# Turning the memory queries with VectorE blocks and an exchange, and issuing two exchanges from GpSimd in four parts

## The chip, the cores and the metric

The kernel runs on one core of a Trainium2 chip. The core's engines run side by side, each through its own list of instructions in order, and wait for one another by semaphores: TensorE (PE; matrix products and its own kind of transpose), VectorE (DVE), ScalarE (ACT), GpSimd (POOL) and SyncE (SP). SyncE and GpSimd issue the DMA transfers of this kernel, each into a queue of its own, and 16 DMA engines carry out both. The metric is the time of one execution on the device in microseconds; lower is better.

## The reference

Two layers of a bidirectional encoder over 512 positions of width 2048. Each layer norms its input, makes one wide input projection, cuts that into the inputs of three parallel groups of heads and a gate, and projects the gated result back:

```python
for l in range(DEPTH):
    h = rmsnorm(x, pre_norm_g[l])
    z = h @ w_in[l]
    q_lat, kv_lat, k_pe, gb, gc, xin, q_mem, gate = split_cols(z)
    ...
    a_out = mla_attention(q, k, v)
    c_out = short_gated_conv(gb, gc, xin, conv_w[l])
    mem_n = rmsnorm(mem, mem_norm_g[l])
    m_out = memory_attention(q_mem.reshape(b, s, MEM_HEADS, MEM_HEAD_DIM), mem_n, w_mk[l], w_mv[l])
    y = jnp.concatenate([a_out, c_out, m_out], axis=-1) * jax.nn.silu(gate)
    o = y @ w_o[l]
    x = x + rmsnorm(o, post_norm_g[l])
```

`memory_attention` takes the queries `q_mem` (512 positions, 4 heads of 128) to 256 memory tokens: scores, softmax, and the weighted sum of the values. `short_gated_conv` is `gb * conv3(gc * xin)`, a convolution of width 3 over positions. All of it is float32.

## The kernel before

**Products.** A float32 matrix is split into a high part and a rest (`wh` and `wl` for weights, lines 189 and 190), and each product is done as three matmuls: high by high, high by rest, rest by high (lines 272 to 274 of `mm3`). TensorE takes the positions in four tiles of 128.

**Input projection.** For each layer it is done in five groups of columns, 0 to 4, each by a scheme with seven products of half-size blocks in place of eight (P1 to P7, called passes). A group needs sums and differences of weight blocks: some are formed on VectorE (line 178), others by loads that add to what lies in the buffer already. The groups that matter here:

- group 2 makes the gate `gm` and the memory queries `qm` (512 columns each);
- group 3, tile `lat`, makes the latents of the multi-head attention, 2 x 416 columns, in 28 steps of one weight tile each (about 281 to 345 us in layer 0 and 1007 to 1071 us in layer 1); VectorE also works out the tables of the rotary positions beside it in layer 0 (`tables`, `tables_wide`, `tables_turned`; lines 327 to 357);
- group 4 makes the gates `ga` (2 x 512 columns; 345 to 432 us and 1071 to 1158 us); beside its later steps the latents are normed and turned.

**Order.** `Program` holds a list of steps: a step names its weight units and a function. `put` adds the steps of passes, `add` a function without weights, and `weave(steps, extra, every, n)` puts n of the extra steps behind every so many steps. In `run` (lines 124 ff.) the loads of weight units run ahead of the step by a fixed number of units: a plain load goes out on SyncE's queue, an accumulating one (`more`, line 146 on GpSimd) goes to GpSimd's, behind the step that has used the buffer's first contents. There are 8 raw buffers `wr`, and 3 each of `wh` and `wl`; a cast waits until one of the three is free, that is until TensorE is through with it. Work on VectorE may be placed by the scheduler a little away from where the program has it; that is seen in the rows below.

**Blocks and exchanges.** Tiles in `BLOCKS` hold a row of positions by channels laid out so that VectorE can turn 32x32 blocks in place (`blocks_turned`, line 935: STREAM_TRANSPOSE). What then is still missing of a whole transpose is a swap of blocks among the four quarters of the partitions; `exchange` (lines 937 to 943) does it with 16 DMAs of 32x4x128 elements, 64 KB each, from the source tile to a slab. `gate_rows` does so for the gates and `conv_rows` for the result of the convolution, `cy`, into a slab `y`. In all of them SyncE issues the DMAs. The convolution ends on VectorE in line 987 (`cy` times `gb`), and its exchange comes into the program behind the third step of group 3.

**Memory queries.** `qm` isn't among the blocks. `qm_turn` (lines 998 to 1006) turns it by TensorE: for each of the four heads four transposes into a PSUM bank (`turn4`, line 917, tile `tps`), from which ScalarE takes the scaled high part `QmH` (line 1004) and VectorE the rest `QmL` (line 1005). The four turns, and seven turns of latents, are woven into group 4, two behind each second step from its seventeenth on.

Of the kernel before, what the change touches and what calls it, by code (L numbers as in the profile page):

```python
# [5 lines left out]
F32 = mybir.dt.float32  # L6
# [52 lines left out]
PI_DOWN = 3.1415925  # L59

RAW, PIECES, SLABS = 8, 4, 19
BLOCKS = "gc", "gb", "gm", "ga0", "ga1"


class Unit:
# [162 lines left out]
def encoder(tc, x, xt, mem, memt, positions, columns, conv_w, w_in, q_norm_g, w_uq, w_qr, kv_norm_g, w_ukv,  # L228
# [32 lines left out]
    def slab(name, dt=F32):  # L261
        return slabs.tile([P, D], dt, tag="slab", name=nm(name))
# [657 lines left out]
    def y_slab(k):  # L920
        if k not in G["ys"]:
            G["ys"][k] = slab("y").rearrange("p (j c) -> p j c", j=4)
        return G["ys"][k]

    def of_tiles(a):

        return a.rearrange("q (t p j) -> q t p j", t=NT, j=32)

    def in_tiles(a):

        return a.rearrange("q (p t j) -> q t p j", t=NT, j=32)
# [2 lines left out]

        nc.vector.transpose(v, v)

    def exchange(dst, src):


        for p in range(4):  # L940
            for b in range(4):
                a = src[32 * p:32 * p + 32].rearrange("i t (c b) j -> i c b (t j)", b=4)[:, :, b]
                nc.sync.dma_start(dst[32 * b:32 * b + 32, :, P * p:P * p + P], a)  # L943

    def gate_rows(k, name, C):
        def f():
# [45 lines left out]
        turns = [turn(n, t) for n in ("gc", "gb") for t in range(NT)]  # L992
        return [[(f, []) for f in fs] for fs in (turns[:4] + [edges] + turns[4:], [part(c) for c in range(8)], [ends])]

    def conv_rows(C):
        return lambda: exchange(y_slab(2), C["cy"])

    def qm_turn(j, C):
        def f():
            if j == 0:  # L1000
                G["Qm"] = tuple(slab(n, F32R).rearrange("p (i c) -> p i c", i=4) for n in ("QmH", "QmL"))
            ps = turn4(lambda t: C["qm"][:, t], j)
            hi, lo = G["Qm"][0][:, j, :], G["Qm"][1][:, j, :]
            nc.scalar.activation(hi, ps, AF.Copy, scale=SC_MEM)
            nc.vector.scalar_tensor_tensor(lo, ps, SC_MEM, hi.bitcast(F32), op0=ALU.mult, op1=ALU.subtract)
        return f

    def normalise(views, n, gain, by=None):
# [177 lines left out]
    def head_iters(j, rope, src, keys, whole=False):  # L1186
# [50 lines left out]
        def av(b):  # L1237
            def g():
                if b == 0 or whole:
                    st["o"] = bank("o")  # L1240
                VH, VL = src()[1]
                o = st["o"] if whole else st["o"][:, b * 256:(b + 1) * 256]
                PT = st.pop("PT" if whole else ("PT", b))
                for k in range(kts):
                    mm3(o, (VH(k), VL(k)), (PT[0][:, k], PT[1][:, k]), k == 0, k == kts - 1)
                if b == 1:
                    y = G["ys"][j // 4][:, j % 4, :]
                    nc.vector.tensor_tensor(in_tiles(y), of_tiles(st["o"]), in_tiles(y), op=ALU.mult)
            return g
        return [((score(t), [], 0.4), trans(t), av(t // 2) if t == 3 or t == 1 and not whole else None, 4 if whole and kts > 2 else 5)  # L1250
                for t in range(NT)]
# [250 lines left out]
    for l in range(depth):  # L1502
# [111 lines left out]
        put(gs[2][1], weave(gs[2][2], turns, 1), weave(gs[2][3] + gs[2][4], parts, 1))  # L1614
        add(owns[3])
        put(gs[3][0][:1], ends, gs[3][0][1:3])
        add(conv_rows(C))
        put(gs[3][0][3:])
        steps = [s for passes in gs[3][1:] for s in passes]
        if l == 0:  # L1620
            add(tables)
            steps[16:16] = [(tables_wide, [])]
            steps[20:20] = [(tables_turned, [])]
        put(steps)
        add(owns[4])
        add(lambda l=l: latents_rows(l))
        g4 = [s for steps in gs[4] for s in steps]
        put(g4[:2])
        add(lambda l=l, C=C: latents_begin(l, C))
        put(g4[2:8])  # L1630
        add(lambda C=C: k_rope(C))
        put(g4[8:13])
        add(gate_rows(3, "gm", C))
        put(g4[13:16])
        lat = [latent_turn(l, "cq", j) for j in range(4)] + [latent_turn(l, "ckv", j) for j in range(2)] + [k_rope_turn]
        more = [(f, []) for f in lat + [qm_turn(j, C) for j in range(4)]]
        put(weave(g4[16:], more, 2, 2)[:-2])
        add(mem_fetch)
        add(tables_fetch)
        put(weave(g4[16:], more, 2, 2)[-2:])  # L1640
        G["left"] = Y = Left(False, l + 1 < depth)
        g0, g1, gains, fetch = out_proj(l)

# [81 lines left out]
```

## Time and profile before

| | |
|---|---|
| time, median of 3 runs | 1462.49 us (1461.67 to 1463.37) |
| time of the profiled execution | 1462.12 us |
| its span | 1460.3 us |
| granted TensorE clock | 0.998 |
| GpSimd busy | 271.1 us (19%) |
| q0, the software queue of GpSimd: packets, MB, share of the 16 engines | 56192, 125.39, 42.6% |
| q1, the hardware queue of SyncE: packets, MB, share of the 16 engines | 105184, 170.74, 36.4% |
| y<-cy, 32 pieces of 64 KB in both layers, issue to landing | 4.5 us (median) |
| y<-gm, 32 pieces, issue to landing | 6.6 us (median) |

The profiled execution's time is 1.8 us more than its span. PE is TensorE's matmuls, PEld its weight loads, which lie beside them; a line such as "L190 DVE" is line 190 of the kernel on VectorE. In the rows of a timeline, the bracket at the end tells how long the engine had idled and what ended that. In rows of waits stand the total, the number of waits and the longest, in us. In rows of windows there follow, behind the stretch and its length, the busy time of PE, PEld, DVE, ACT and POOL with counts, the granted clock, the busy share of the DMA engines (1.00 is all 16) and GB/s. "SPq" is time in which SyncE issues DMAs.

### The profile page before, as it was taken

Reading aid. Unit: us, or ns where it says so; the run is one execution under the profiler, and the core shown is the slowest. Engines: PE = TensorE matmul, PEld = TensorE weight load, DVE = VectorE, ACT = ScalarE, POOL = GpSimd, SP = SyncE. Lnnn points to the kernel's source line nnn. Section 1 sums busy time; section 2 is a strip of 40 time slices with the busy share of each in tenths; the row PEclk is TensorE's granted clock in tenths of the full one; section 3 lists DMA queues with packets and bytes.
Section 4 is the critical chain, followed back from the end, with each engine's and each line's share of the span. In section 5 each row is a group of like instructions: output and inputs, shape, how many; then the busy total and the mean of one; then the engine's idle time right before and its main releaser. Section 6 shows DMA issues by size and latency. Waiting matters only on the chain.

```text
span 1460.3 us, 19491 instructions
## 1 busy us (share of the span) xinstructions
PE 1444.3 (99%) x7040; PEld 1231.5 (84%) x7040; DVE 1108.3 (76%) x1529; ACT 870.4 (60%) x1350; POOL 271.1 (19%) x280
## 2 busy tenths in 40 slices
PE   9999999999999999999999999999999999999997
PEld 8888888898888888888898888888988888888886
DVE  5899685977678778868879666759576776788687
ACT  7856344636468688644777434445364686776543
POOL 0032303031301100311210333030313001004111
PEclk9999999999999999999999999999999999999999
DMA  9999969697976382795986999695979664129973
GB/s 368 415 260 220 231 185 206 156 207 215 235 220 181 83 264 87 135 242 148 340 286 224 240 233 227 187 193 157 215 197 239 219 179 114 31 87 159 269 164 130
DMA packets 161472, 297.37 MB, mean 204 GB/s; under 512 B 12288, under 2 KB 51744, under 8 KB 157536
## 3 DMA queue, kind: packets, MB, share of 16 engines
q0 software_dynamic: 56192, 125.39, 42.6%
q1 hardware_dynamic: 105184, 170.74, 36.4%
q8 instruction: 55, 0.90, 0.2%
q14 instruction: 41, 0.34, 0.1%
HBM read 266.05 MB, written 21.63 MB: 197 GB/s over the span
## 4 chain that ended last, share of the span: by engine, by line
PE 89%; DVE 4%; DMA 2%; SPq 2%; issue 1%; ACT 1%; POOL 0%; POOLq 0%; DVEq 0%; ACTq 0%
PE P L273 21%; PE P L274 21%; PE P L272 21%; PE ptp L1233 2%; DVE wl L190 2%; SPq L943 2%; DMA wr<-in_w_in_dram 2%; PE o L273 1%; PE o L272 1%; PE o L274 1%; PE sc L272 1%; PE sc L273 1%; PE sc L274 1%; PE mk L274 1%; PE mk L273 1%
## 5 line engine op out<-in xcount | busy, mean ns | idle before, releaser
L189 ACT CAST wh<-wr 128x1024 fp32r<-128x1024 f32 (+2 forms) x436 | 444.3, 1023 | 438.8 <-PE P L274 311.5
L190 DVE TENSOR_TENSOR wl<-wr,wh 128x1024 fp32r<-128x1024 f32 (+2 forms) x436 | 515.2, 1185 | 240.6 <-ACT wh L189 237.5
L272 PE MATMUL P<-wh,S 128*128 128x512 f32 (+1 forms) x896 | 344.5, 384 | 0.8 <-DVE lat L542 0.4
L273 PE MATMUL P<-wl,S 128*128 128x512 f32 (+1 forms) x896 | 343.6, 384 | 0.6 <-DVE wl L190 0.6
L274 PE MATMUL P<-wh,S 128*128 128x512 f32 (+1 forms) x896 | 343.8, 384 | 0.0
L272 PE MATMUL P<-wh,A 128*128 128x512 f32 (+1 forms) x656 | 252.9, 386 | 2.0 <-ACT wh L189 2.0
L273 PE MATMUL P<-wl,A 128*128 128x512 f32 (+1 forms) x656 | 252.1, 384 | 2.5 <-DVE wl L190 2.5
L274 PE MATMUL P<-wh,A 128*128 128x512 f32 (+1 forms) x656 | 251.8, 384 | 0.0
L146 POOL DMA_DIRECT2D wr<-in_w_in_dram x132 | 158.2, 1198 | 438.8 <-DVE wl L190 258.4
L272 PEld LDWEIGHTS P<-wh,S 128*128 128x128 f32 x896 | 168.2, 188 | 31.5 <-DVE lat L542 0.8
L273 PEld LDWEIGHTS P<-wl,S 128*128 128x128 f32 x896 | 168.2, 188 | 31.0 <-DVE wl L190 0.9
L274 PEld LDWEIGHTS P<-wh,S 128*128 128x128 f32 x896 | 168.2, 188 | 30.0
L273 PEld LDWEIGHTS P<-wl,A 128*128 128x128 f32 x656 | 123.2, 188 | 25.5 <-DVE wl L190 3.7
L272 PEld LDWEIGHTS P<-wh,A 128*128 128x128 f32 x656 | 123.1, 188 | 24.5 <-ACT wh L189 2.7
L274 PEld LDWEIGHTS P<-wh,A 128*128 128x128 f32 x656 | 123.1, 188 | 22.1
L146 POOL DMA_DIRECT2D wr<-in_w_o_dram x40 | 48.3, 1235 | 299.7 <-DVE wl L190 292.8
L1220 ACT ACTIVATE P<-sc,nm 128x512 f32<-128x512 f32 (+1 forms) x96 | 59.9, 624 | 27.7 <-DVE nm L1217 27.4
L1223 ACT ACTIVATE P<-P,rec 128x512 f32<-128x512 f32 (+1 forms) x96 | 62.3, 662 | 7.0 <-DVE rec L1222 7.0
L1217 DVE TENSOR_REDUCE nm<-sc 128x1 f32<-128x512 f32 (+1 forms) x96 | 56.7, 595 | 10.0 <-PE sc L1215 9.0
L178 DVE TENSOR_TENSOR wr<-wr,wr 128x1024 f32<-128x1024 f32 (+1 forms) x36 | 42.3, 1175 | 5.5 <-DMA wr<-in_w_in_dram 5.1
L1233 PE MATMUL ptp<-identr,P 128*128 128x128 f32 x320 | 46.0, 272 | 0.3 <-ACT P L1223 0.3
L1233 PEld LDWEIGHTS ptp<-identr,P 128*128 128x128 f32 x320 | 38.0, 140 | 6.5 <-ACT P L1223 0.7
(323 smaller groups left out, 2081.2 us busy)
## 6 DMA issues: line engine op xcount, KB each, us to landing
wr<-in_w_in_dram SPq DMA_DIRECT2D x128, 512.0 KB, 5.6
wr<-in_w_in_dram POOLq DMA_DIRECT2D x108, 512.0 KB, 7.3
wr<-in_w_o_dram SPq DMA_DIRECT2D x48, 512.0 KB, 6.1
wr<-in_w_o_dram POOLq DMA_DIRECT2D x40, 512.0 KB, 7.2
wr<-in_w_in_dram SPq DMA_DIRECT2D x32, 416.0 KB, 3.8
wr<-in_w_in_dram POOLq DMA_DIRECT2D x24, 416.0 KB, 6.9
wr<-in_w_mk_dram SPq DMA_DIRECT2D x15, 512.0 KB, 8.7
wr<-in_w_mv_dram SPq DMA_DIRECT2D x15, 512.0 KB, 10.1
```

The lines of the kernel that those rows point to most:

```text
L146: engine.dma_start(dst, src, **kw)
L178: nc.vector.tensor_tensor(tiles[a], tiles[a], tiles[b], op=ALU.add)
L189: pin(nc.scalar.copy(hi[:, h], src[:, h]))
L190: pin(nc.vector.tensor_tensor(lo[:, h], src[:, h], hi[:, h].bitcast(F32), op=ALU.subtract))
L272: nc.tensor.matmul(ps, ah, bh, start=first, stop=False, **kw)
L273: nc.tensor.matmul(ps, ah, bl, start=False, stop=False, **kw)
L274: nc.tensor.matmul(ps, al, bh, start=False, stop=last, **kw)
L943: nc.sync.dma_start(dst[32 * b:32 * b + 32, :, P * p:P * p + P], a)
L1217: nc.vector.tensor_reduce(nmax, ps, axis=AX.X, op=ALU.max, negate=True)
L1220: nc.scalar.activation(pt, ps, AF.Exp, bias=nmax, accum_out=tot)
L1223: nc.scalar.activation(pt, pt, AF.Copy, scale=rec)
L1233: nc.tensor.transpose(ps[:, k * P:(k + 1) * P], pt[:, k * P:(k + 1) * P], G["ident"])
```

## The change

Five things are changed in the program of each layer.

1. `qm` joins the blocks. VectorE turns its blocks in place with four transposes of 128x512 (`qm_turn(t, C)`), put at steps 11 to 17 of group 3's later passes, and 16 exchange DMAs bring them into a slab (`qm_rows`), which is also the one that will hold the rest part `QmL`. They are issued by GpSimd in four parts of four, between steps of group 4. Two splits of 1024 columns each (`qm_split`) then take the high and the rest part from that slab in SBUF; the 16 transposes on TensorE and their evictions are gone.
2. The convolution's exchange is issued by GpSimd too, in four parts of four, at the start of group 3.
3. The latent turns and the two splits are woven one behind each step of group 4, and no longer two behind each second one.
4. Two functions of the rotary tables come later among group 3's steps (`tables_wide` from 16 to 22, `tables_turned` from 20 to 26; the six steps put in ahead of them are four block turns and two parts of the exchange, which leaves the two functions within a step of where they were among the weight steps; in VectorE's own order the rope terms of lines 327 to 357 begin two rests `wl` later).
5. The last multiplication of the memory heads by the gate takes `y` as contiguous rows.

```diff
-BLOCKS = "gc", "gb", "gm", "ga0", "ga1"
+BLOCKS = "gc", "gb", "gm", "qm", "ga0", "ga1"
...
-    def exchange(dst, src):
+    def exchange(dst, src, queue=nc.sync, blocks=range(4)):
-        for p in range(4):
+        for p in blocks:
             for b in range(4):
                 a = src[32 * p:32 * p + 32].rearrange("i t (c b) j -> i c b (t j)", b=4)[:, :, b]
-                nc.sync.dma_start(dst[32 * b:32 * b + 32, :, P * p:P * p + P], a)
+                queue.dma_start(dst[32 * b:32 * b + 32, :, P * p:P * p + P], a)
...
-    def conv_rows(C):
-        return lambda: exchange(y_slab(2), C["cy"])
-    def qm_turn(j, C):
+    def conv_rows(p, C):
+        return lambda: exchange(y_slab(2), C["cy"], nc.gpsimd, (p,))
+    def qm_turn(t, C):
+        return lambda: blocks_turned(C["qm"][:, t])
+    def qm_rows(p, C):
         def f():
-            if j == 0:
-                G["Qm"] = tuple(slab(n, F32R).rearrange("p (i c) -> p i c", i=4) for n in ("QmH", "QmL"))
-            ps = turn4(lambda t: C["qm"][:, t], j)
-            hi, lo = G["Qm"][0][:, j, :], G["Qm"][1][:, j, :]
-            nc.scalar.activation(hi, ps, AF.Copy, scale=SC_MEM)
-            nc.vector.scalar_tensor_tensor(lo, ps, SC_MEM, hi.bitcast(F32), op0=ALU.mult, op1=ALU.subtract)
+            if p == 0:
+                C["QmL"] = slab("QmL")
+            exchange(C["QmL"].rearrange("p (i c) -> p i c", i=4), C["qm"], nc.gpsimd, (p,))
+        return f
+    def qm_split(k, C):
+        def f():
+            if k == 0:
+                G["Qm"] = slab("QmH", F32R), C["QmL"]
+            h, (hi, lo) = slice(1024 * k, 1024 * k + 1024), G["Qm"]
+            nc.scalar.activation(hi[:, h], lo[:, h], AF.Copy, scale=SC_MEM)
+            nc.vector.scalar_tensor_tensor(lo[:, h].bitcast(F32R), lo[:, h], SC_MEM, hi[:, h].bitcast(F32),
+                                           op0=ALU.mult, op1=ALU.subtract)
+            if k:
+                G["Qm"] = tuple(a.rearrange("p (i c) -> p i c", i=4) for a in (hi, lo.bitcast(F32R)))
         return f
...
-                    nc.vector.tensor_tensor(in_tiles(y), of_tiles(st["o"]), in_tiles(y), op=ALU.mult)
+                    if rope is None:
+                        nc.vector.tensor_tensor(y, st["o"], y, op=ALU.mult)
+                    else:
+                        nc.vector.tensor_tensor(in_tiles(y), of_tiles(st["o"]), in_tiles(y), op=ALU.mult)
...
-        add(conv_rows(C))
+        add(conv_rows(0, C))
         put(gs[3][0][3:])
+        add(conv_rows(1, C))
         steps = [s for passes in gs[3][1:] for s in passes]
+        for n in (17, 15, 13, 11):
+            steps[n:n] = [(qm_turn((17 - n) // 2, C), [])]
+        steps[2:2] = [(conv_rows(3, C), [])]
+        steps[1:1] = [(conv_rows(2, C), [])]
         if l == 0:
             add(tables)
-            steps[16:16] = [(tables_wide, [])]
-            steps[20:20] = [(tables_turned, [])]
+            steps[22:22] = [(tables_wide, [])]
+            steps[26:26] = [(tables_turned, [])]
...
-        put(g4[2:8])
+        put(g4[2:6])
+        add(qm_rows(0, C))
+        put(g4[6:8])
+        add(qm_rows(1, C))
         add(lambda C=C: k_rope(C))
-        put(g4[8:13])
+        put(g4[8:10])
+        add(qm_rows(2, C))
+        put(g4[10:12])
+        add(qm_rows(3, C))
+        put(g4[12:13])
...
-        more = [(f, []) for f in lat + [qm_turn(j, C) for j in range(4)]]
-        put(weave(g4[16:], more, 2, 2)[:-2])
+        more = [(f, []) for f in lat[:4] + [qm_split(0, C)] + lat[4:6] + [qm_split(1, C)] + lat[6:]]
+        last = weave(g4[16:], more, 1)
+        put(last[:-2])
```

What this moves is seen in the order of the instructions. On SyncE, at the start of group 3 in layer 0 (`wr` are raw weight buffers, loaded 416 columns wide; `y<-cy` is the convolution's exchange), as a piece of the difference:

```order
 L146 DMA wr_2452<-in_w_in_dram 128x2x416
 L146 DMA wr_2470<-in_w_in_dram 128x2x416
-L943 DMA y_2490<-cy_2164 32x4x128 x16
-L146 DMA wr_2507<-in_w_in_dram 128x2x416
-L146 DMA wr_2562<-in_w_in_dram 128x2x416
+L146 DMA wr_2495<-in_w_in_dram 128x2x416
+L146 DMA wr_2558<-in_w_in_dram 128x2x416
```

The weight loads now follow one another; the numbers of the buffers change only in name. On GpSimd at the same place, where the `wr` rows are accumulating loads:

```order
 L146 DMA wr_2041<-in_w_in_dram 128x2x512
 L146 DMA wr_2222<-in_w_in_dram 128x2x416
+L943 DMA y_2490<-cy_2164 32x4x128 x8
 L146 DMA wr_2246<-in_w_in_dram 128x2x416
+L943 DMA y_2490<-cy_2164 32x4x128 x8
 L146 DMA wr_2270<-in_w_in_dram 128x2x416
 L146 DMA wr_2294<-in_w_in_dram 128x2x416
```

The four parts stand as two lots of eight, ahead of the second and of the third accumulating load of group 3. In group 4 of layer 0, still on GpSimd, the queries' exchange stands so in the changed kernel:

```order
L146 DMA wr_2906<-in_w_in_dram 128x2x512
L943 DMA QmL_3208<-qm_1831 32x4x128 x4
L146 DMA wr_2924<-in_w_in_dram 128x2x512
L943 DMA QmL_3208<-qm_1831 32x4x128 x4
L146 DMA wr_2959<-in_w_in_dram 128x2x512
L943 DMA QmL_3208<-qm_1831 32x4x128 x4
L146 DMA wr_2883<-in_w_in_dram 128x2x512
L146 DMA wr_3188<-in_w_in_dram 128x2x512
L943 DMA QmL_3208<-qm_1831 32x4x128 x4
L146 DMA wr_2906<-in_w_in_dram 128x2x512
```

Before, these accumulating loads followed one another without anything between them; now a part of four stands ahead of the third, fourth, fifth and seventh load of the group. On VectorE, where group 3 of layer 0 begins, the rows before were (`wl` are rests of weight tiles, written wl_2429 and so on, which TensorE takes in that order; line 178 sums two raw tiles; line 935 turns blocks):

```order
L190 TENSOR_TENSOR wl_2373<-wr_2222,wh_2372 128x832
L987 TENSOR_TENSOR cy_2164<-cy_2164,gb_867 128x1024
L190 TENSOR_TENSOR wl_2397<-wr_2246,wh_2396 128x832
L178 TENSOR_TENSOR wr_2222<-wr_2222,wr_2322 128x832
L935 STREAM_TRANSPOSE gm_1830<-gm_1830 128x16x32
L178 TENSOR_TENSOR wr_2246<-wr_2246,wr_2370 128x832
L935 STREAM_TRANSPOSE gm_1830<-gm_1830 128x16x32
L190 TENSOR_TENSOR wl_2429<-wr_2270,wh_2428 128x832
L190 TENSOR_TENSOR wl_2455<-wr_2294,wh_2454 128x832
```

and in the changed kernel they are:

```order
L190 TENSOR_TENSOR wl_2373<-wr_2222,wh_2372 128x832
L984 TENSOR_TENSOR cy_2164<-cy_2164,ends_2157 128x16
L935 STREAM_TRANSPOSE qm_1831<-qm_1831 128x16x32
L987 TENSOR_TENSOR cy_2164<-cy_2164,gb_867 128x1024
L190 TENSOR_TENSOR wl_2397<-wr_2246,wh_2396 128x832
L987 TENSOR_TENSOR cy_2164<-cy_2164,gb_867 128x1024
L935 STREAM_TRANSPOSE gm_1830<-gm_1830 128x16x32
L178 TENSOR_TENSOR wr_2222<-wr_2222,wr_2322 128x832
L935 STREAM_TRANSPOSE gm_1830<-gm_1830 128x16x32
L190 TENSOR_TENSOR wl_2429<-wr_2270,wh_2428 128x832
L190 TENSOR_TENSOR wl_2455<-wr_2294,wh_2454 128x832
L178 TENSOR_TENSOR wr_2246<-wr_2246,wr_2370 128x832
```

Two of the four new transposes of `qm` stand here (the first just ahead of wl_2373), one multiplication of line 987 has moved behind wl_2397, and one sum of line 178 behind wl_2455, the third and fourth rests of the group being wl_2429 and wl_2455. The other two transposes come among the next five rests.

## The prediction on record

> **What bounds the kernel now.** I read first the page's busy times, its chain that ended last and its costliest groups, then what TensorE waited for, in the two stretches where the change works: the tail of the conv and memory group and the latent group that follows it (280 to 345 us in layer 0, 1005 to 1072 us in layer 1).
>
> ```profile
> PE 1444.3 (99%) x7040; PEld 1231.5 (84%) x7040; DVE 1108.3 (76%) x1529; ACT 870.4 (60%) x1350; POOL 271.1 (19%) x280
> PE 89%; DVE 4%; DMA 2%; SPq 2%; issue 1%; ACT 1%; POOL 0%; POOLq 0%; DVEq 0%; ACTq 0%
> PE P L273 <- DVE wl L190: 1.2, 2, 0.6
> PE P L272 <- ACT wh L189: 1.1, 1, 1.1
> PE P L272 <- DVE lat L542: 0.4, 1, 0.4
> ...
> PE P L273 <- DVE wl L190: 1.9, 3, 0.7
> PE P L272 <- ACT wh L189: 1.3, 2, 0.9
> ```
>
> TensorE is busy for 99% of the span, so time can go only where its own instructions go or where it waits. The waits rows (total, times, longest) of layer 0 stand above the dots, those of layer 1 below: TensorE waits for the high part (wh) or the low part, the rest (wl), of a weight tile. The chain through these stretches shows why:
>
> ```profile
> 288.67 13.56 SPq L943 DMA_DIRECT2D y<-cy  x16
> 302.33 4.64 DMA wr<-in_w_in_dram
> 307.08 0.89 ACT wh L189
> 307.99 1.03 DVE wl L190
> 309.07 0.45 PE P L273
> 309.53 0.19 PE P L274
> ```
> ```profile
> 1014.77 13.48 SPq L943 DMA_DIRECT2D y<-cy  x16
> 1028.35 4.35 DMA wr<-in_w_in_dram
> 1032.80 0.89 ACT wh L189
> 1051.96 9.48 DMA wr<-in_w_in_dram
> 1061.54 0.90 ACT wh L189
> ```
>
> SyncE spends 13.56 us issuing the 16 pieces of the conv exchange. The weight load queued behind them starts only at 302.33, lands after 4.64 us, and ScalarE casts at once: the load is what is late. In layer 1 the same, and 20 us later a second wait: an accumulating load of GpSimd, issued at 1051.96, needs 9.48 us, and the cast at 1061.54 starts on its landing.
>
> **Removed: the turns on TensorE.** Chain pieces of layer 0, and the tile view's row of both layers:
>
> ```profile
> 417.93 0.46 PE tps L917 x4
> 423.85 0.87 PE tps L917 x8
> 430.21 0.44 PE tps L917 x4
> L917 PE MATMUL tps<-identr,qm x32: 270/272/296, 417.8 to 1156.1; 128*128 128x128 f32 x32
> ```
>
> Sixteen turns hold TensorE for 0.46 + 0.87 + 0.44 = 1.77 us, 0.11 each in the pipeline (the 272 ns of one overlap the next). Nothing else holds it there, so all counts: 2 x 1.77 = **-3.5 us**.
>
> **Removed: the late loads.** With the exchange off SyncE's queue, the load at 302.33 can go about 13 us earlier, long before its cast is due. Idle time that ended there: 1.1 + 0.6 us in layer 0, and, at every restart, the first matmul takes 0.45 where the next takes 0.19, so 0.26 more, twice: 2.2 us. In layer 1 the two late loads have both waits for high parts, 1.3, and two of the three for low parts, two thirds of 1.9 or 1.27; with four restarts 1.3 + 1.27 + 1.04 = 3.6. Together **-5.8 us**, if the loads behind then come in time. That is the weakest step, since the exchange's bytes still move, now on GpSimd's queue, where the accumulating loads go:
>
> ```profile
> 307.08 2.46 ACT L189 CAST wh<-wr 128x832 fp32r<-128x832 f32 x3 [6.06 <-DMA wr<-in_w_in_dram]
> 334.97 1.67 ACT L189 CAST wh<-wr 128x832 fp32r<-128x832 f32 x2 [4.48 <-DMA wr<-in_w_in_dram]
> 1032.80 1.67 ACT L189 CAST wh<-wr 128x832 fp32r<-128x832 f32 x2 [5.80 <-DMA wr<-in_w_in_dram]
> 1061.54 2.46 ACT L189 CAST wh<-wr 128x832 fp32r<-128x832 f32 x3 [5.34 <-DMA wr<-in_w_in_dram]
> ```
> ```profile
> 310.00:330.00 20.00, 19.59 (x105) 19.05 (x103) 19.41 (x56) 8.94 (x13) 9.48 (x8) 1.00 1.10 205
> 370.00:385.00 15.00, 15.00 (x68) 12.43 (x67) 9.02 (x10) 7.87 (x10) 4.35 (x4) 1.00 1.10 274
> 385.00:412.00 27.00, 27.00 (x133) 22.61 (x132) 17.39 (x20) 13.15 (x17) 8.38 (x8) 1.00 1.11 252
> 1010.00:1015.00 5.00, 4.26 (x23) 3.88 (x22) 5.00 (x6) 1.21 (x3) 0.00 (x0) 1.00 0.60 170
> ```
>
> In brackets is how long ScalarE idled before a cast for a landing. At 5.34 to 6.06 us TensorE waited, at 4.48 it did not: three buffers of split weights cover between 4.5 and 5.3 us of lateness. The DMA column of the windows (last but one; the engines' busy times stand ahead of it in the order TensorE, weight loads, VectorE, ScalarE, GpSimd) is full at 1.10 from 310 to 330. Had the accumulating loads landed no sooner, removing 2.2 us ahead of them would turn the 4.48 of layer 0 into 6.7 and the gain would be given back. I expect them sooner, since they are started by what the late load held up:
>
> ```profile
> 297.96 1.18 POOL L146 DMA_DIRECT2D wr<-in_w_in_dram  x1 [2.46 <-DVE wl L190]
> 302.51 1.17 POOL L146 DMA_DIRECT2D wr<-in_w_in_dram  x1 [3.36 <-DVE wl L190]
> 310.51 1.17 POOL L146 DMA_DIRECT2D wr<-in_w_in_dram  x1 [6.83 <-DVE rti L338]
> L1125 POOL DMA_DIRECT2D QR<-qrd x16 | 8.8, 554 | 10.5 <-DMA qrd<-rm 3.7 <-issue 2.0 <-PE sc L1215 1.8
> ```
>
> Between 302.51 and 310.51 GpSimd idles for 6.83 us behind low parts that come late with that load. The row QR<-qrd is the nearest to a piece of an exchange on GpSimd (as many rows, four times the length): 554 ns, so 16 pieces take 8.9 us of GpSimd, in two lots of 8, one ahead of the load before that of 297.96 and one ahead of 297.96 itself. The loads go out up to 2 x 4.4 us later, and the idle 6.83 swallows nearly all: by the load of 310.51 the queue is level or ahead. Bounds: nothing given back, or all 5.8.
>
> **Added: block turns on VectorE.** Four transposes per layer, two of them ahead of the third and fourth low parts of group 3, for one of which TensorE already waits (the first wl wait of each layer; VectorE 5.00 of 5 us busy at 1010):
>
> ```profile
> 282.28 1.02 DVE L178 TENSOR_TENSOR wr<-wr,wr 128x832 f32<-128x832 f32 x1
> 283.21 0.70 DVE L935 STREAM_TRANSPOSE gm<-gm 128x512 f32<-128x512 f32 x1
> 283.84 0.98 DVE L178 TENSOR_TENSOR wr<-wr,wr 128x832 f32<-128x832 f32 x1
> ```
>
> From start to start a transpose costs 0.63 and a weight sum 0.93. Two transposes come ahead, one sum goes behind: 2 x 0.63 - 0.93 = 0.33 per layer, **+0.7 us**. Bounds: none of it (VectorE catches up), or the whole 1.26 per layer, 2.5. The other two fall behind those waits where VectorE so far idled for the late load; at nothing, as long as VectorE's 19.41 of 20 us from 310 to 330, with the rope terms two steps later, doesn't stretch the 0.4 wait on lat: 0 to 1.6.
>
> For four 128x128 tiles the rows give TensorE 1.77/4 = 0.44 us and VectorE 0.63, and the exchange on top. The Trainium skill ("VectorE: DVE Perf Modes", § Rules for kernel authors) says to use TensorE for a 128x128 transpose if its destination may be PSUM. Taken as a price list, that makes the swap a loss of 4 x (0.63 - 0.44) = 0.8 us a layer, 1.5 in place of the gain of 3.5; this trace agrees on the order of the two, but has TensorE at 99% and VectorE at 76%, so I count what TensorE gets back. By the price list the time would be 1453.9 + 3.5 + 1.5 = 1458.9, the worse end of the third rival.
>
> **Added: the query exchange in group 4.** 16 pieces in four parts between accumulating loads. At 64 KB each they are 1.05 MB, about 3.8 us of DMA at the 274 GB/s of the window 370 to 385, an estimate. DMA is full there (1.10, 1.11), so the loads behind come up to 3.8 us later. What they have:
>
> ```profile
> 409.35 1.05 ACT L189 CAST wh<-wr 128x1024 fp32r<-128x1024 f32 x1 [1.63 <-DMA wr<-in_w_in_dram]
> 1134.60 1.05 ACT L189 CAST wh<-wr 128x1024 fp32r<-128x1024 f32 x1 [1.20 <-DMA wr<-in_w_in_dram]
> ```
>
> At worst the cast idles 1.63 + 3.8 = 5.4 us. Group 4's tiles are 1024 wide instead of 832, so three buffers cover 1024/832 times as much, 5.5 to 6.5 us, an estimate. **0 us**, bounds 0 and 2 per layer. The splits become two of 1024 per engine instead of four of 512, off the path. The memory heads' multiply takes as many elements as before, off the path: 0. Weaving the latent turns one per step instead of two per two moves TensorE work, not its amount: 0.
>
> **Sum.** -3.5 - 2.2 - 3.6 + 0.7 = -8.6 from the profiled execution's 1462.1 us (span 1460.3): 1453.5. The median of the runs is 0.4 above that execution, so **1453.9 us**.
>
> **Rivals.**
> *The accumulating loads pay.* The bytes are the same and DMA is full from 310 on; what SyncE no longer delays, GpSimd does. For it: the 9.48 us landing at 1051.96, and 1.10. Against: the idle 6.83 us above. Full return of 5.8: 1459.7; half: 1456.8. The Trainium skill has this rival's rule ("DMA: Bandwidth & Descriptors", § Issuing engines are not separate DMA queues): all issuers share the same 16 engines, and another issuer saves only issue time, usually small. Here that issue time is 13.56 us, so I give the full return 0.1, the half 0.1.
>
> *VectorE becomes the bound.* The turns aren't offset by the moved sum (2 x 0.93 more) and the lat wait grows by 1.6: 3.5 us on top, 1457.4. For it: 5.00 of 5. Chance 0.12.
>
> *The turns' 3.5 us isn't gained,* because in group 4 the steps without them outrun the casts and TensorE waits instead: 1457.4. Against it, the casts mostly wait for TensorE, not TensorE for them:
>
> ```profile
> L189 ACT CAST wh<-wr 128x1024 fp32r<-128x1024 f32 (+2 forms) x436 | 444.3, 1023 | 438.8 <-PE P L274 311.5
> ```
>
> Of the 438.8 us that ScalarE idles before casts, 311.5 end on TensorE. Chance 0.05.
>
> *Slower: GpSimd stalls in group 4.* GpSimd issues in order. If a piece must wait for an earlier transfer to land before it can be issued, as long as the 9.48 us seen in layer 1, the accumulating load behind it is late by 1.63 + 9.48 + 3.8 = 14.9 us, over what three buffers cover (5.5 at the least) by 9.4, in each layer 9.4: 1453.9 + 18.8 = 1472.7. It decides from 5.5 us of lateness, and makes the kernel slower than before from 5.5 + 8.6/2 = 9.8. Against: GpSimd is busy 8.38 of 27 us there. Chance 0.09.
>
> **How the numbers follow.** Forecast (1450.8 to 1456) 0.54; the rest 0.46 as above. The low end takes the forecast without the VectorE term and without the three waits that I left in (0.4, 0.6, 0.63, and 0.26 for each restart): 1453.9 - 0.7 - 2.4 = 1450.8. The high end takes in the full return: 1460.0. Left out are the slow rival and some outer ends, under 0.2. A measurement here can tell about 0.2%, 2.9 us, from no change. Faster by more (under 1459.6): 0.54 + 0.12 + 0.05 + 0.1 = 0.81; within: the full return, 0.1; slower: 0.09.
>
> **What would show it.** The conv exchange in GpSimd's rows, SyncE's weight loads without the 13 us hole, and no ScalarE idle over 5 us before casts at 300 to 310 and 1030 to 1065: right about the loads. TensorE's waits for the high parts, 1.1 and 1.3, gone, or come back near 335 and 1060: the rival. The first wl wait of each layer up by 0.33: the VectorE term. Casts at 400 to 415 idling over 5.5 us for a landing, or GpSimd's group 4 loads issued ten us later: slower. No tps<-qm rows, with 3.5 us less of TensorE: the turns.

## The result, and the profile after

The changed kernel is slower: 1474.8 us (median of 4 runs, 1471.5 to 1477.6) against 1462.3 us (4 runs), a ratio of 1.0084 with a 95% interval of 1.0062 to 1.0106. The forecast was 1453.9 us, range 1450.8 to 1460.0. The profiled execution of the changed kernel took 1477.58 us, its span is 1475.8 us; that of before took 1462.12 us with 1460.3 us. So the rows below have 15.5 us to explain, somewhat more than the medians' 12.5.

The page of the changed kernel, its busy times and the chain that ended last, by engine:

```profile
PE 1448.5 (98%) x7008; PEld 1231.3 (83%) x7008; DVE 1111.2 (75%) x1533; ACT 869.7 (59%) x1346; POOL 308.0 (21%) x344
...
PE 82%; DMA 7%; DVE 6%; issue 2%; POOL 1%; ACT 1%; SPq 1%; POOLq 0%; DVEq 0%; ACTq 0%
```

The 32 turns are gone from TensorE (7008 matmuls for 7040), and yet TensorE holds 82% of the chain instead of 89%; DMA and VectorE have what it lost. TensorE's waits over the whole execution (total us, times, longest):

```profile
PE P L273 <- DVE wl L190: 8.6, 12, 1.6
PE P L272 <- ACT wh L189: 4.3, 2, 3.6
PE P L272 <- DVE lat L542: 4.2, 1, 4.2
```

That is 17.1 us in 15 waits, against 5.9 us in 9 before (3.1, 2.4 and 0.4). What was 3.1 for the rests is 8.6, and there are two long waits: 4.2 us for the eviction of a latent in layer 0, and 3.6 us for a high part in layer 1. Where they come from is seen on GpSimd. Its timeline at the start of group 3 in layer 0 (start, length, instruction, count, idle time before and what ended it):

```profile
291.57 1.18 POOL L146 DMA_DIRECT2D wr<-in_w_in_dram  x1 [34.78 <-DVE wl L190]
292.32 4.30 POOL L943 DMA_DIRECT2D y<-cy  x7
300.19 0.55 POOL L943 DMA_DIRECT2D y<-cy  x1 [3.57 <-DMA wr<-in_w_in_dram]
300.98 1.23 POOL L146 DMA_DIRECT2D wr<-in_w_in_dram  x1 [0.23 <-issue]
301.71 4.34 POOL L943 DMA_DIRECT2D y<-cy  x7
309.40 0.56 POOL L943 DMA_DIRECT2D y<-cy  x1 [3.35 <-DMA y<-cy]
309.96 3.71 POOL L146 DMA_DIRECT2D wr<-in_w_in_dram  x3
```

Seven pieces go out in 4.3 us, as forecast. Then GpSimd stands for 3.57 us: the eighth piece may not be issued before the transfer eight issues back, the accumulating load of 291.57, has landed, 8.6 us after its issue. (In the trace GpSimd's DMAs signal on eight semaphores in turn, and each issue waits for the one that it will use.) The second lot stands for 3.35 us in the same way, for the load of 300.98; the row names a piece that landed just then. So the third accumulating load, which went out at 297.96 before, goes out at 309.96, and the last piece of the exchange, issued at 309.40, lands at 313.3, nearly 12 us after its lot began. Now the user of the exchange's source. The first rope term on VectorE, in the timeline before and after:

```profile
304.41 0.68 DVE L327 TENSOR_SCALAR ropescr<-inv,posf 128x32 f32<-128x32 f32 x4 [2.34 <-DMA y<-cy]
```
```profile
313.42 0.68 DVE L327 TENSOR_SCALAR ropescr<-inv,posf 128x32 f32<-128x32 f32 x4 [2.93 <-DMA y<-cy]
```

The rope terms have nothing to do with `y` or `cy`. They write a scratch slab, all 19 slabs are in use, and the one they get is `cy`'s, which is free only when every piece of the exchange has been read out. They also stand two rests later in VectorE's order than before, but the row shows what releases them: VectorE idles 2.93 us for the landing. They start 9 us later, VectorE works without a gap from 318 to 338 us, and the latent's eviction in its queue comes late: TensorE's 4.2 us. In layer 1 there are no rope terms, and there ScalarE's copy into the second latent slab takes `cy`'s place. ScalarE's rows, the copy before, which waits for nothing, and then the changed kernel's:

```profile
1034.38 0.91 ACT L571 COPY lat<-P 128x416 f32<-128x416 f32 x2
```
```profile
1046.40 0.91 ACT L571 COPY lat<-P 128x416 f32<-128x416 f32 x2 [4.78 <-DMA y<-cy]
...
1074.62 2.46 ACT L189 CAST wh<-wr 128x832 fp32r<-128x832 f32 x3 [7.21 <-DMA wr<-in_w_in_dram]
```

The copy waits 4.78 us for the exchange, and three casts are queued behind it. At 1074.62 an accumulating load is late by 7.21 us, over the 4.5 to 5.3 that three buffers cover. That load went out at 1064.64; GpSimd had issued the last piece of the exchange at 1042.64, so these rows don't show what made it late (see e14).

A last row comes with the long waits. The windows around them (length, busy us of PE, PEld, DVE, ACT and POOL, granted clock, DMA share, GB/s), two of before and then those of the changed kernel:

```profile
320.00:340.00 20.00, 19.59 (x107) 19.03 (x106) 15.36 (x36) 9.93 (x15) 4.82 (x6) 1.00 0.96 211
1060.00:1080.00 20.00, 18.99 (x94) 17.35 (x94) 13.29 (x13) 13.95 (x27) 1.64 (x3) 1.00 0.73 232
```
```profile
320.00:340.00 20.00, 15.75 (x77) 14.52 (x76) 17.83 (x51) 6.65 (x10) 6.10 (x6) 0.95 1.08 221
340.00:360.00 20.00, 20.00 (x105) 19.33 (x104) 11.70 (x12) 12.23 (x21) 1.16 (x2) 0.96 0.68 203
1060.00:1080.00 20.00, 16.05 (x75) 15.06 (x74) 8.90 (x12) 5.63 (x7) 3.65 (x3) 0.88 0.88 201
1080.00:1100.00 20.00, 20.00 (x94) 18.15 (x93) 13.69 (x14) 13.56 (x27) 3.77 (x5) 0.95 0.64 196
```

Behind the two long waits the clock is below 1.00, in the kernel before it was not anywhere in these windows. What is missing, 20 x (0.05 + 0.04 + 0.12 + 0.05), is 5.2 us of full clock. In finer windows it is 0.50 from 338.1 to 341.4 us and from 1075.6 to 1082.0, so hardly any of that lies in the waits themselves, which end at 337.05 and 1075.56.

A sum for the profiled execution: waits +11.2, six more restarts at 0.26 each +1.6, clock +5, turns -3.5, together 14.3 of the 15.5 us. I don't place the rest.

### The profile page after: what moved, and what is told of

It is laid out like the page before. It is cut to its first block, busy times and chain, and to the rows that moved or that the text cites. A ratio compares the mean times of both kernels' runs of the same rounds, so it can differ in the third digit from the quotient of the medians.

```text
span 1475.8 us, 19493 instructions
## 1 busy us (share of the span) xinstructions
PE 1448.5 (98%) x7008; PEld 1231.3 (83%) x7008; DVE 1111.2 (75%) x1533; ACT 869.7 (59%) x1346; POOL 308.0 (21%) x344
## 4 chain that ended last, share of the span: by engine, by line
PE 82%; DMA 7%; DVE 6%; issue 2%; POOL 1%; ACT 1%; SPq 1%; POOLq 0%; DVEq 0%; ACTq 0%
PE P L273 18%; PE P L274 18%; PE P L272 18%; DVE wl L190 3%; DMA wr<-in_w_in_dram 2%; PE ptp L1245 2%; DMA y<-cy 2%; DMA y<-gm 2%; PE o L273 1%; PE o L274 1%; PE o L272 1%; PE sc L272 1%; PE sc L273 1%; PE sc L274 1%; POOL wr L146 1%
```

## The experiments

The ratio is to the kernel before, run beside each on the same chip. It took 1462.3 us beside the changed kernel and 1460.4 to 1460.9 us beside the others, so only ratios are compared. Each kernel has one profile.

| kernel | ratio, 95% interval | wait for lat, layer 0 |
|---|---|---|
| changed | 1.0084 (1.0062 to 1.0106) | 4.2 us |
| e1: conv exchange back on SyncE, one piece | 1.0048 (1.0029 to 1.0067) | 1.4 |
| e2: before, conv exchange alone moved | 1.0046 (1.0029 to 1.0063) | 4.3 |
| e3: conv exchange in parts on SyncE | 1.0058 (1.0039 to 1.0076) | 4.2 |
| e4: both exchanges in parts on SyncE | 1.0052 (1.0033 to 1.0070) | 4.2 |
| e5: rope scratch off the slab | 1.0041 (1.0026 to 1.0056) | none |
| e9: before, cy's slab held | 1.0076 (1.0056 to 1.0096) | 3.8 |
| e7: e1 with turns pinned | 1.0017 (1.0002 to 1.0032) | 2.5 |
| e8: e1 with turns in group 4 | 1.0010 (0.9997 to 1.0022) | 0.4 |
| e14: changed, turns in group 4 | 1.0067 (1.0047 to 1.0087) | 4.3 |
| e11: e8, query exchange late | 0.9991 (0.9979 to 1.0002) | 0.5 |
| e13: before, conv exchange on both queues | 0.9986 (0.9977 to 0.9995) | none |
| e12: e11, conv exchange on both queues | 0.9974 (0.9963 to 0.9985) | none |

**Which half of the change costs it: e1 to e4.** Theory A blames the convolution's exchange, theory B the query turns and their exchange.

```diff
# e1, against the changed kernel
-        add(conv_rows(0, C))
+        add(lambda C=C: exchange(y_slab(2), C["cy"]))
         put(gs[3][0][3:])
-        add(conv_rows(1, C))
...
-        steps[2:2] = [(conv_rows(3, C), [])]
-        steps[1:1] = [(conv_rows(2, C), [])]
```

> The changed kernel, with the convolution's exchange issued by SyncE again, 16 pieces in one go at its old place; the memory queries still by VectorE blocks and GpSimd's exchange. Theory A (the convolution's exchange on GpSimd costs the time: GpSimd stands for the landing of the accumulating loads eight issues back, so the exchange lands late, holds the slab of cy that the rope terms and the latents' copies need next, and pushes the accumulating loads of group 3 back): time falls to 1459 to 1464, that is before's 1462.3 less 3.5 for the turns, plus about 1.7 for the first rests of group 3 and up to 2 in group 4; no TensorE wait over 2 us. Theory B (the query turns on VectorE and their exchange cost it): stays at 1471 or more, and the long waits at 337 and 1075 us stay.

e2 takes only that part of the change into the kernel before: `conv_rows(p, C)` with `nc.gpsimd` at the same four places.

> The kernel before with the convolution's exchange alone moved to GpSimd in its four parts; the queries turned by TensorE as before. Theory A: slower than before by 8 to 13 us, 1470 to 1476, with waits of 3 us and more at 335 to 340 and 1060 to 1080 us, and a granted clock under 0.97 behind them. Theory B: about 1457 to 1460, since only the late loads of SyncE go.

Each half alone costs about the same, 1.0048 and 1.0046, so A and B as stated are both half right: e1 stayed above A's 1464 (5.5 us over its reference instead of 1.7 at most), e2 came out below A's 1470. They add up to about the whole. e2 is also the prediction's step on the late loads by itself: 6.7 us slower (4.2 to 9.2), where 5.8 us faster was forecast. e1 has no wait over 1.5 us and a clock of 1.00; its cost lies in the rests at the start of group 3 (below). In e2 the wait for the latent is there, 4.3 us, with a clock of 0.91 behind it:

```profile
320.00:340.00 20.00, 15.74 (x74) 14.71 (x73) 15.85 (x44) 6.65 (x10) 4.72 (x4) 0.91 0.93 198
```

In layer 1 e2 has no long wait: 1.3 us in all between 1005 and 1072 us, where before had 3.2.

```diff
# e3, against the changed kernel (e4 does the same in qm_rows too)
-        return lambda: exchange(y_slab(2), C["cy"], nc.gpsimd, (p,))
+        return lambda: exchange(y_slab(2), C["cy"], nc.sync, (p,))
```

> The changed kernel with the convolution's exchange in its four parts at the new places, but issued by SyncE. Theory A (the queue counts, not the parts): 1456 to 1461: no standing of GpSimd, and no weight load of SyncE waits behind more than eight pieces (5 us). Theory B: 1470 or more. Theory A2 (parts count: weight loads behind each part still come late): 1460 to 1465, like one piece.

> Both exchanges in their four parts issued by SyncE. Against the kernel with only the convolution's on SyncE this tells what the query exchange costs on GpSimd in group 4, whose waits of 0.4 and 0.5 us (layer 0) and 1.2 and 0.3 us (layer 1) then go: theory A 2 us faster than that kernel, 1454 to 1459. Rival: SyncE's own weight loads for the next stage come late instead: same or slower.

Both are misses for A, and e3 for A2 too; e4 came out as its rival had it. By the number alone e3 is theory B's (1.0058 of 1462.3 is 1470.8), but e1 and e2 had already put about half of the loss on each side. On SyncE nothing stands for the accumulating loads, and yet the wait for the latent is 4.2 us: it doesn't need GpSimd's standing. The first rope term of e3:

```profile
312.61 0.67 DVE L327 TENSOR_SCALAR ropescr<-inv,posf 128x32 f32<-128x32 f32 x4
```

It starts nearly as late as in the changed kernel, but VectorE has not idled before it; it has just ended a rest. SyncE had issued the last piece by 305.28, and it landed at 309.2. So in e3 no landing starts the terms late but their place in VectorE's order, behind later rests than before; in the changed kernel and in e2 it is the landing. What all three share is that the rope terms come late, and the next runs are about the slab that they need. Between e3 and e4 there is no difference that the intervals separate, so putting the query exchange on SyncE too doesn't tell what it costs.

**The slab: e9 and e5.** e9 does nothing but hold the slab, in the kernel before:

```diff
+        def hold(l=l, C=C):
+            junk = dram.tile([32, 512], F32, name=f"junk{l}")
+            nc.gpsimd.dma_start(junk, C["slab", "y"][96:128, :512])
+        steps[6:6] = [(hold, [])]
```

> The kernel before with one extra DMA of 64 KB in each layer, from cy to a spare place in DRAM, issued by GpSimd behind the fourth accumulating load of group 3 (nothing reads it): all it does is to give cy's slab back later, by some 4 to 6 us; everything else stays. Theory A: TensorE's wait on the latent's eviction in layer 0 grows from 0.4 to 1.5 to 4.3 us, the rope terms start at 308 us or later, and the time goes up by 2 to 6 us. Theory B: no change beyond 1 us.

One extra DMA per layer makes it 1.0076, 11 us, more than the 2 to 6 expected; the size was missed, the sign and place were not. Its rows:

```profile
311.39 0.68 DVE L327 TENSOR_SCALAR ropescr<-inv,posf 128x32 f32<-128x32 f32 x4 [2.69 <-DMA wr<-in_w_in_dram]
```
```profile
PE P L272 <- DVE lat L542: 3.8, 1, 3.8
```
```profile
320.00:340.00 20.00, 16.22 (x80) 15.62 (x79) 17.19 (x50) 7.13 (x11) 5.53 (x5) 0.93 1.02 215
```

The rope terms start at 311.39 instead of 304.41. The extra DMA goes out at 303.35 and takes 8.0 us to land, and the first term waits for its semaphore; the row names a load that landed about then. The wait and the lower clock follow, with the conv exchange itself untouched. TensorE's waits are 10.4 us instead of 5.9, and the clock is at 0.50 for three stretches of 3.4 us (from 313.2, 337.1 and 1043.7 us), which costs 5.1 us more: 9.6 in all, where the two spans differ by 9.2. The extra DMA is also one more issue on GpSimd, but the next load there waits for a rope term on VectorE, not for it.

e5 takes the rope scratch out of the slab, in the changed kernel, and leaves all the rest:

```diff
-            v["scr"] = slab("ropescr").rearrange("p (i n) -> p i n", n=n)
+            one, two = (scrap(k).rearrange("p (i n) -> p i n", n=n) for k in ("ropea", "ropeb"))
+            v["scr"] = [one[:, 0], one[:, 1], one[:, 2], one[:, 3], two[:, 0], two[:, 1]]
+            v["a1"], v["ti"] = two[:, 2].bitcast(F32R), two[:, 3].bitcast(I32)
```

> The changed kernel, with the rotary tables' scratch put into two of the small pieces instead of a slab, so that VectorE's rope terms no longer need the slab that the convolution's exchange reads (cy). Theory A (that slab, given back only when the exchange has landed, starts the rope terms at 313 us instead of 304 and so makes TensorE wait 4.2 us for a latent's eviction in layer 0, with a clock of 0.95 behind): that wait goes or shrinks under 2 us, and the ratio to before falls from 1.0084 to about 1.004 to 1.006; the second latent slab of layer 0 now takes cy's place and may wait 1 to 2 us. Theory B (GpSimd's late accumulating loads alone): the wait in layer 0 stays at 4 us.

1.0041: half of the loss is gone, and so is the wait on line 542. With the slab the terms lose their late place in VectorE's order too (those of lines 327 to 356 are done at 309.5 us), so e5 takes away both; e9 is the run that holds the slab alone. What stays are waits for high parts whose accumulating loads are late, 2.3 us at 335 us (the cast idles 6.74 us) and 3.5 us in layer 1. That GpSimd's standing makes these loads late is not shown (see e14).

**The turns ahead of the rests: e7, e8 and e14.**

```diff
# e7, against e1
-        return lambda: blocks_turned(C["qm"][:, t])
+        return lambda: pr.pin(nc.vector.transpose(C["qm"][:, t], C["qm"][:, t]))
# e8, against e7; the four insertions among group 3's steps go
-        put(g4[2:6])
+        for k in range(4):
+            put(g4[2 + k:3 + k])
+            add(qm_turn(k, C))
```

> The kernel with the convolution's exchange back on SyncE in one piece and the query turns by VectorE, but with the four turns held in the order of the program, so that none is pulled ahead of the first rests of group 3. Theory C (the turns ahead of the rests and sums cost 1.7 us in layer 0 and 2.1 in layer 1, the waits at 287, 300, 1004, 1016 and 1028 us): these go back to before's 0.7 and 0.9; the time falls from 1.0048 of before to 1.001 to 1.003. In layer 0 two turns now lie among the last rope terms and can lengthen the wait for the latent there by up to 1.3 us.

> As the one before, but with the four turns held among the first steps of group 4, behind the rope terms. Theory C: group 3 is then the same as in the kernel before, TensorE is without 3.5 us of turns, and the time is 0.997 to 0.999 of before, less what the query exchange costs in group 4 (0.4 us of waits in the kernel with the exchange in one piece). Rival: the queries' exchange itself, by its bytes or by GpSimd's time, costs the 3.5 us again: 1.000 or more.

> The changed kernel with nothing altered but the place of the four query turns, held among the first steps of group 4; the convolution's exchange on GpSimd in its four parts, the queries' exchange between the accumulating loads. If the causes add (A for the convolution's exchange, C for the turns ahead of the rests), the ratio is 1.0084 less the 0.0038 that the same move gave with the exchange on SyncE: 1.004 to 1.006; the waits at 301 and 1034 us go, that of 4.2 us for the latent in layer 0 stays, and so does layer 1's long wait for an accumulating load if GpSimd's standing makes it. If the turns had made layer 1's long wait by shifting the first steps, it shrinks below 1.5 us.

From e1 to e7 and e8 the ratio falls by 0.003 and 0.004, 4.5 to 5.5 us, each to within some 3.5 us: theory C holds in size. In e7 the waits of layer 0 between 284 and 304 us go from 2.1 us back to 0.8, those of layer 1 between 1000 and 1032 us only from 2.5 to 1.5 (before 0.7), and the wait for the latent grows from 1.4 to 2.5 us, as was expected. VectorE's rows of the changed kernel show why so much comes from four transposes of 0.63 us:

```profile
291.12 1.02 DVE L178 TENSOR_TENSOR wr<-wr,wr 128x832 f32<-128x832 f32 x1
292.06 0.70 DVE L935 STREAM_TRANSPOSE qm<-qm 128x512 f32<-128x512 f32 x1
292.69 0.98 DVE L190 TENSOR_TENSOR wl<-wr,wh 128x832 fp32r<-128x832 f32 x1
293.59 0.70 DVE L935 STREAM_TRANSPOSE qm<-qm 128x512 f32<-128x512 f32 x1
294.42 1.03 DVE L190 TENSOR_TENSOR wl<-wr,wh 128x832 fp32r<-128x832 f32 x1
299.61 1.03 DVE L178 TENSOR_TENSOR wr<-wr,wr 128x832 f32<-128x832 f32 x1 [4.16 <-DMA wr<-in_w_in_dram]
300.55 2.89 DVE L190 TENSOR_TENSOR wl<-wr,wh 128x832 fp32r<-128x832 f32 x3
```

The last sum of these stood so in the kernel before:

```profile
291.92 1.03 DVE L178 TENSOR_TENSOR wr<-wr,wr 128x832 f32<-128x832 f32 x1 [1.12 <-DMA wr<-in_w_in_dram]
```

The sums of line 178 give raw buffers back to SyncE's loads. The first three start at 285.89, 289.25 and 291.12 us, before at 282.28, 283.84 and 287.20, so I take it that a load goes out later; the next sum waits 4.16 us for its load, and three rests are queued behind that sum. With the turns pinned that wait falls from 4.05 us (e1) to 1.02 (e7). In the changed kernel TensorE waited 3.1 us in two waits between 284 and 304 us, before 0.6 in one.

In e8 the turns add no waits in group 3 (2.8 and 3.2 us in the two layers, before 2.7 and 3.2), but its 1.0010 is above the 0.997 to 0.999 expected; the rival had it. The waits that it has over before are in group 4. (The profiled execution, 1466.73 us, is 3.7 us over the median of e8's runs, so its rows show more loss than is usual; one stretch of 3.4 us at half clock lies in group 3, at 309.8 us.) TensorE's wait there, ScalarE's casts before it, and the clock, in layer 1 of e8:

```profile
PE P L273 <- DVE wl L190: 1.8, 1, 1.8
```
```profile
1137.20 1.05 ACT L189 CAST wh<-wr 128x1024 fp32r<-128x1024 f32 x1 [4.00 <-DMA wr<-in_w_in_dram]
```
```profile
1140.00:1160.00 20.00, 18.21 (x81) 14.89 (x81) 14.25 (x17) 11.60 (x16) 0.53 (x1) 0.91 0.91 303
```

The cast idles only 4.00 us, less than what three buffers should cover. But a latent's copy is woven behind each cast now, on ScalarE and then on VectorE, and there the rest that TensorE needs stands behind it and behind two block turns of `ga`:

```profile
1138.76 0.69 DVE L278 TENSOR_TENSOR cqL<-tps,cqH 128x512 fp32r<-128x512 f32 x1 [3.54 <-ACT cqH L277]
1139.37 1.29 DVE L935 STREAM_TRANSPOSE ga<-ga 128x512 f32<-128x512 f32 x2
1140.59 1.18 DVE L190 TENSOR_TENSOR wl<-wr,wh 128x1024 fp32r<-128x1024 f32 x1
```

So the cover was shorter than the casts alone say.

e14 is e8's move made in the changed kernel: 1.0067, a fall of 0.0017 where 0.0038 was expected; the intervals exclude neither that nor no change at all. The waits of the latent (4.3 us) and of layer 1's accumulating load (3.1 us) stay. e14's expectation laid the second to GpSimd's standing, but that doesn't fit: in layer 1 GpSimd stands only 0.69 and 1.29 us in e14, and e2, where it stands 0.62 and 1.68 us, has no such wait (the cast there idles 4.94 us, which the buffers cover). What makes that load late stays open.

**The query exchange behind the loads, and the conv exchange on two queues: e11, e13, e12.**

```diff
# e11, against e8: qm_rows leaves its four places; both(a, b) calls a and b
+        fs = lat[:5] + [both(lat[5], qm_rows(0, C)), qm_rows(1, C), both(lat[6], qm_rows(2, C)), qm_rows(3, C)]
+        more = [(f, []) for f in fs]
...
+        add(qm_split(0, C))
+        add(qm_split(1, C))
# e12 (against e11) and e13 (against the kernel before)
+        def both_queues(C=C):
+            exchange(y_slab(2), C["cy"], nc.gpsimd, (0, 1))
+            exchange(y_slab(2), C["cy"], nc.sync, (2, 3))
+        add(both_queues)
```

> The kernel with the query turns held in group 4 and the convolution's exchange in one piece on SyncE, but with the queries' exchange issued by GpSimd in one go behind the last accumulating load of group 4, and both splits behind it. Theory D (in group 4 the exchange between the accumulating loads makes the last ones about 5 us later, from which come the TensorE waits of 1.2 and 2.0 us at 414 and 1142 us and the lower clock behind the second): these waits go, and the time is 0.996 to 0.9985 of before (the turns' 3.5 us). Rival: the exchange now runs into the loads of the next stage or the splits come too late for the memory heads: 0.999 to 1.002, with new waits at 425 to 450 and 1155 to 1180 us.

> The kernel before with nothing changed but the convolution's exchange shared out on both queues in the same way. Theory A: 3 to 5 us faster than before, 0.9965 to 0.998. Rival: within 1 us of before.

> As the one before, with the convolution's exchange shared out at its old place: eight pieces issued by GpSimd, eight by SyncE, at once. Theory A (what counts is when the last piece has landed and cy's slab is free, and how long SyncE's weight loads stand behind): SyncE's hole falls from 13.5 to about 6.5 us, the exchange lands no later than before, the waits at 308 and 1035 us shrink: 3 to 5 us faster than the kernel before this one, 0.993 to 0.996 of before. Rival: GpSimd's eight pieces delay the accumulating loads instead: no faster than the kernel before this one.

e11 is at 0.9991, 0.002 below e8, and its waits in group 4 are gone: theory D holds in direction. Its size is the rival's, though without the new waits that the rival named. The 3.5 us of the turns would be 0.9976, just under the interval's lower edge; less than half of it (1.3 us) is what is measured, and the interval doesn't exclude zero. e13 is 0.9986 and e12 0.9974, faster than the kernel before and the changed one, though each by less than was expected. (The profiled execution of e12, 1452.69 us, is 4.2 us under the median of its runs.) e12's timelines, SyncE, GpSimd and VectorE:

```profile
289.03 7.05 SPq L943 DMA_DIRECT2D y<-cy  x8
```
```profile
290.63 4.30 POOL L943 DMA_DIRECT2D y<-cy  x7
296.15 0.55 POOL L943 DMA_DIRECT2D y<-cy  x1 [1.22 <-DMA y<-cy]
```
```profile
299.65 0.68 DVE L327 TENSOR_SCALAR ropescr<-inv,posf 128x32 f32<-128x32 f32 x4 [1.76 <-DMA wr<-in_w_in_dram]
```

SyncE's hole is 7.05 us in place of 13.56, GpSimd stands for 1.22 instead of 3.57, and the rope terms begin at 299.65, earliest of the kernels that keep them in the slab. TensorE's waits for weights in the input projection are two in the whole of e12:

```profile
PE P L273 <- DVE wl L190: 1.3, 2, 0.7
```

## Why the prediction was wrong

- **Turns off TensorE, -3.5 us:** right as a row (32 matmuls fewer). e11, where most of the rest is out of the way, gives -1.3 us, with an interval from -3.1 to +0.3: short of -3.5, and not clear of zero.
- **Late loads, -5.8 us: the step that failed.** e2, which makes this step alone, is 6.7 us slower (4.2 to 9.2). The late weight loads of SyncE did go (its ten loads follow one another from 276.73 us, without the hole of 13.56), but the conv exchange's own landing was taken to matter to nobody. The prediction priced its pieces at 8.9 us of GpSimd and let an idle 6.83 us swallow that. Two things were left out. GpSimd stood 3.57 and 3.35 us for landings eight issues back, so the third accumulating load was 12 us late, not level. And the exchange's source slab is what the rope terms (layer 0) and a latent's copy (layer 1) wait for: e9 shows that holding that slab alone costs 11 us (the waits of TensorE come in layer 0; neither e2 nor e9 has a long one in layer 1). The row that tells it was in the trace of before: the rope terms at 304.41 idled 2.34 us for `y<-cy`. And the 6.83 us that were to swallow the pieces ended, by their own row, on a rope term (`rti`), not on a rest. The bound of this step, "nothing given back, or all 5.8", was too narrow, because it was made from the waits that were there and not from those that could come.
- **Block turns ahead of the rests, +0.7 us:** too small. By e1, e7 and e8 they cost 4.5 to 5.5 us, to within some 3.5, against a bound of 2.5. The step counted the sum that moves behind as 0.93 us gained; it was the sum that frees a load's buffer, and the rests behind the next sum waited for that load. The half of the change without the conv exchange, forecast at -2.8 us, came out 7.0 us slower (e1).
- **Query exchange in group 4, 0 us, at most 2 per layer:** not nothing, but within the bounds: moving it out of the way gave 2.8 us for both layers (e8 to e11). The estimate of the cover, 5.5 us, was wrong: 4.00 us of idle time was enough for a wait of 1.8.
- **The rival of the paying loads** had its sign seen: TensorE's waits for high parts were to come back near 335 and 1060 us, and did, 2.3 us at 335 and 3.5 us at 1062 in e5 and 3.6 us at 1072 in the changed kernel. It gave back 5.8 us at most, since it counted only the waits that were there.
- **The rival of VectorE as the bound** had the right wait, that for the latent, but let it grow by 1.6 us at most; it grew by 3.8.
- **The slower rival:** its mechanism, a piece that must wait for an earlier landing with the accumulating load behind it, is what GpSimd's rows show. It stands so in group 4 as well (3.27 us in layer 1), with little behind it; the cost came in group 3. It had a chance of 0.09 and was sought in group 4, though the conv exchange has the same form and larger lots.
- **The clock** had no term at all. The Trainium skill ("TensorE: Matmul & The Clock Gate", § HAM oscillation) warns of idle gaps of TensorE over some 3.4 us, behind which it runs at half rate for a while. The trace agrees on the half rate: behind the 4.2 us wait a matmul takes 0.35 us and 3 us later 0.19. It doesn't agree on the 3.4 us: in e8 half rate followed a wait of 1.8 us. The rows of the changed kernel:

```profile
338.66 0.35 PE P L272
...
341.69 0.19 PE P L272
```

- **Issuing from two engines.** The Trainium skill ("DMA: Bandwidth & Descriptors", § Issuing engines are not separate DMA queues) says that a second issuer saves only issue time, usually small. The prediction weighed it beside the rival that gives the gain back. Here that time is 13.56 us of SyncE's queue, and sharing the same 16 DMAs between two issuers gives 0.9986 by itself (e13), while giving all of them to GpSimd gives 1.0046 (e2).

## What to carry to other kernels

Before a transfer is moved, look up who gets its source buffer next, by the rows in which an engine idles for that transfer, and price the landing of its last piece, not its issue. An engine that issues DMAs in order stands for the landing of the one a full rotation back (eight issues in this kernel): small pieces mixed with slow accumulating loads inherit the slow ones' latency. And an operation that frees a buffer for a load, when it moves back, can cost not its own length but the wait for that load.

## What the runs showed of the hardware that was not expected

The granted clock fell after waits of TensorE, and by more than their length tells. In these traces, away from the first and last 10 us of an execution, it is either 1.00 or 0.50, and 0.50 for 3.4 us or twice that at a time; a stretch of 3.4 us costs 1.7 us. All ten waits of 2.5 us or more in these kernels have such a stretch that begins within 2 us of their end. Shorter ones don't sort by length. Waits of 1.8 us (e8, rows above) and 2.0 us (e9) had one, and so had 1.1 us in e8 (at 308 us; 0.50 from 309.8) and 0.9 us in e9 (at 1042 us; 0.50 from 1043.7). But 2.3 us in e5 (at 336 us) had none, nor had 1.6 us in the changed kernel at 301 us or the 1.1 us of before at 307. What decides it isn't shown, and there is one profile of each kernel. It is why holding one slab could cost 11 us with 4.5 us of additional waits.
